# Two scales for the first range of w1, loaded and used half by half, in a two-phase MLP on one Trainium2 core

## The chip, the cores and the metric

The kernel runs on one core of a Trainium2 chip. The metric is the device time of one execution in microseconds (us). The kernel before the change took 1545.94, 1545.28 and 1545.81 us in three runs; the median is 1545.81.

## What is computed

Three float32 arrays go in: x (8 x 1024 x 1024, so 8192 rows of 1024), w1 (1024 x 4096) and w2 (4096 x 1024).

```python
h = x @ w1
h = 0.5 * h * (1 + np.tanh(np.sqrt(2 / np.pi) * (h + 0.044715 * h ** 3)))
return (h @ w2).astype(np.float32)
```

## The kernel before

**Engines.** TensorE (PE) does the matmuls, each with a 128x128 tile of weights. VectorE (DVE), ScalarE (ACT) and GpSimd (POOL) do everything between them, and SyncE (SP) issues most DMAs. Every engine works through its own instructions in the order in which the program gives them; the kernel uses a manual schedule, so this order is the order of the calls in the code. `V`, `S` and `G` are DVE, ACT and POOL, and `cast(eng, out, in, scale)` (L168-174) is a multiplication by a scale on one of the three.

**Data.** The 8192 rows are 64 chunks c of 128 rows, taken as 32 pairs k (chunks 2k and 2k+1). A chunk of x is loaded (`load_x`, L180), looked at by ACT for the sum of its absolute values in each row (`look_x`), given a scale `xm` and its inverse `xi` per row (`scale_x`), cast to f16 with it (`cast_x`, tile `x16`), and turned into `xT`. For the first twelve chunks TensorE does the turn (`turn_x_pe`, L204-218: eight matmuls into PSUM and a copy out by ACT or DVE); for the others a DMA does.

The columns of w1 are cut into four ranges r. A range has 512 columns in the left half of w1 (column block 0, in the code s=0) and 512 in the right half (block 1, s=1). It comes as eight tiles n of 128x2x512 float32: n0 to n3 hold block 0 (as B11 and B21), n4 to n7 block 1 (B12 and B22). Every tile is looked at (`look_w1`, L266), the maximum over the eight is taken per partition and written into a 128x128 tile `spread` (`widest_w1`), and a matmul called `rows` turns that, so that a reduction gives the maximum over all partitions (`all_partitions`, L154-160). From this come one scale `w1m`, its inverse `w1i` and `w1j` for the whole range (`scale_w1`, L278-282). Then `cast_w1` (L284-288) casts the eight tiles to f16 with `w1i`, and `sum_w1` (L290) forms the sums T1 to T4 of the four blocks B11, B21, B12, B22.

**First phase: gelu(x @ w1).** There are 128 units, one for each pair and range. The order (L576-578) takes the first six pairs (`FIRST`) through range 0, then through ranges 1, 2 and 3; then come 22 middle pairs, each with all four ranges, and the last four pairs range by range. Units 0 to 6 (pairs 0 to 5 with range 0, and pair 0 with range 1) are `Plain` (L426-443): four quarters of one half (128 rows) and one column block each, eight matmuls of 512 columns to a quarter. I call these quarters p0 to p27. The other units are `Quad1` (L445-503, called by `unit`, L694-732): seven products of four matmuls by Strassen's scheme, which need the sums of w1 above and four sums of the pair's `xT` (`sum_x`, L220-234, tile `xs`). In a unit, ACT and DVE copy and add PSUM banks into tiles `e`, ACT applies the gelu with a per-row factor `us`, POOL multiplies by a per-row factor `rs` and casts to f16 (tile `g`, L172), and SP stores `g` to DRAM (`gd`) some calls later (`held`, `let_go`). The two factors are products of the x scale and the scale of the range (`factors`, `factors_of_pair`).

**Second phase: g @ w2.** `second(n)` (L557-571) does the next n of 26 products per pair (eight matmuls of 256 columns each). Their left operands are tiles `gT`, loaded from `gd` by transposing DMAs (`load_g`), and sums `gs` of them on DVE (`sum_g`, L517). After a product ACT or DVE takes the PSUM bank into the output tile, once or twice (`take`, L522-544). The right operands are sums of w2 that the first phase computed, stored in DRAM and fetched again. w2's scale allows for the scales of the ranges of w1 (`widest_w2`, `scale_w2`), and `cast_w2` uses the entry of `w2s` of the range in question.

**Where the phases meet.** A `Quad1` unit finishes its last products in the next two calls of `unit`. In the calls for units 128 and 129 there is no new unit; there `extra(0)` stands in the place of product m1 and `extra(1)` in that of m5, and they call `second` for three and two products (L786) and for three and three (L787).

**Order of the other work.** All else (loads, looks, casts, sums) is put by hand into slots: `plan(u, slot, f)` has `f` called in unit u's slot 0 to 6, and `early(p, f)` (L594) plans for slot p % 4 of unit p // 4, that is, after quarter p. `background` calls what was planned. Each instruction then stands in its engine's queue behind all that was called before it.

**Start.** L740-773 loads x0, x1, the eight tiles of range 0 and x2 to x7 on SP's queue in that order; looks at, casts and turns x0 and x1; gives TensorE 30 warm-up matmuls of 256 columns (`warm_up`, L376, `WARM`), whose results nobody uses; looks at the eight tiles, runs `rows` and the scale, gives 16 more warm-ups, casts the eight tiles (six on DVE, two on ACT) and x2 and x3 on DVE; and then runs the seven plain units, with pair 0's quarters in the order of the column blocks and the other pairs' in that of the halves.

**Tiles.** `wpool` has 28 buffers of 4 KB per partition shared by raw and cast w1, early x and w2's products; `k2` has eleven for `e`, `x16`, `junk`, `g2` and `gs`; PSUM has three banks of each of `pa` and `pc` and two of `pb`, which the turns and `rows` use too.

Of the kernel before, what the change touches and what calls it, by code (L numbers as in the profile page):

```python
# [78 lines left out]
def kernel(  # L79
# [24 lines left out]
    WARM = 30  # L104
# [21 lines left out]
    w1a = small.tile([P, NR], F32, name="w1a")  # L126
    w1m = small.tile([P, NR], F32, name="w1m")
    w1i = small.tile([P, NR], F32, name="w1i")
    w1j = small.tile([P, NR], F32, name="w1j")
# [5 lines left out]
    w2s = small.tile([P, NR], F32, name="w2s")  # L135
    us = small.tile([P, NP, 2, NR], F32, name="us")
    rs = small.tile([P, NP, 2, NR], F32, name="rs")

    ones = small.tile([P, P], F32, name="ones")
# [11 lines left out]
    def spread_out(src):  # L151
        V.tensor_scalar(out=spread, in0=ones, scalar1=src, scalar2=None, op0=ALU.mult)
# [34 lines left out]
    def scale_x(c):  # L187
        V.tensor_scalar(
            out=xm[:, c:c + 1], in0=xl[:, c:c + 1], scalar1=2.0 ** -13, scalar2=TINY,
            op0=ALU.mult, op1=ALU.max,  # L190
        )
        V.reciprocal(xi[:, c:c + 1], xm[:, c:c + 1])
# [43 lines left out]
    def times(o, a, s):  # L236
        V.tensor_scalar(out=o, in0=a, scalar1=s, scalar2=None, op0=ALU.mult)
# [7 lines left out]

    def factors_of_pair(k):
        for h in range(2):
            times(us[:, k, h, :], w1m, xm[:, 2 * k + h:2 * k + h + 1])
            times(rs[:, k, h, :], w1j, xi[:, 2 * k + h:2 * k + h + 1])
# [24 lines left out]
    def widest_w1(r):  # L274
        V.tensor_reduce(out=w1a[:, r:r + 1], in_=w1c[:, r, :], op=ALU.max, axis=AX.X)
        spread_out(w1a[:, r:r + 1])

    def scale_w1(r):  # L278
        all_partitions(w1m[:, r:r + 1])
        V.tensor_scalar_max(w1m[:, r:r + 1], w1m[:, r:r + 1], TINY)  # L280
        V.reciprocal(w1i[:, r:r + 1], w1m[:, r:r + 1])
        V.tensor_scalar_mul(w1j[:, r:r + 1], w1i[:, r:r + 1], 1.0 / SPAN)

    def cast_w1(r, n, eng):  # L284
# [3 lines left out]
        cast(eng, w1set[r, b][:, 2 * half:2 * half + 2], wraw.pop((r, n)), w1i[:, r:r + 1])  # L288
# [23 lines left out]
    def widest_w2():  # L312
        V.tensor_reduce(out=w2m, in_=w2c, op=ALU.max, axis=AX.X)
        V.tensor_tensor(out=w2m, in0=w2m, in1=w1m, op=ALU.mult)
# [72 lines left out]
    class Out1:  # L387


        def begin(self, k, r):  # L390
            self.k, self.r = k, r
            self.u = [us[:, k, h, r:r + 1] for h in range(2)]
            self.v = [rs[:, k, h, r:r + 1] for h in range(2)]
# [6 lines left out]
        def gelu_pair(self, half, s, src):  # L400
            e = self.e()
            S.activation(out=e, in_=src, func=ACT.Gelu_apprx_tanh, scale=self.u[half])
# [3 lines left out]
            cast(G, g[:, s], e, self.v[half])  # L406
# [19 lines left out]
    class Plain(Out1):  # L426
# [4 lines left out]
        def run(self, banks, step):  # L431
            t = xT[self.k]
            for i, (half, s) in enumerate(((0, 0), (0, 1), (1, 0), (1, 1)) if self.k else ((0, 0), (1, 0), (0, 1), (1, 1))):
                ps = bank(banks[i])
                bs = (B12, B22) if s else (B11, B21)
                for j, b in enumerate(bs):
                    product(
                        ps, lambda n: t[:, half, j * HK + n, :],
                        [w1set[self.r, b][:, n, :] for n in range(HK)], j == 0,
                    )  # L440
                self.gelu_pair(half, s, ps)
                step(i)
                let_go(len(held) - 1 if len(held) > 1 and i % 2 else 0)
# [153 lines left out]
    for k in range(1, FIRST):  # L597
        for h in range(2):
            c = 2 * k + h
            if k > 1:  # L600
# [4 lines left out]
                if h:  # L605
                    early(p, factors, k, k + 1, 0)
# [87 lines left out]
    def unit(u, extra):  # L694
# [35 lines left out]
        if p1:  # L730
            p1.m4()
# [90 lines left out]
```

## Time and profile before

| | |
|---|---|
| three runs | 1545.94, 1545.28, 1545.81 us |
| the profiled execution | 1545.54 us |
| its span (first to last instruction) | 1543.8 us |
| PE busy | 1521.1 us (99% of the span), 10415 matmuls |
| PE weight loads | 1015.8 us (66%) |
| DVE busy | 1171.7 us (76%) |
| ACT busy | 731.5 us (47%) |
| POOL busy | 461.9 us (30%) |
| HBM | 97.0 MB read, 114.3 MB written, 137 GB/s over the span |

In the profile's rows a group reads: time or count, engine, line of the kernel, operation, tile written <- tiles read, partitions x elements and type, count. In brackets stands how long the engine had been idle just before and what ended that wait. Times are us from the start of the span unless they are durations. Matmul instructions that overlap with the next are counted once in busy time, so I judge TensorE by the distance from one start to the next. "Granted clock" 1.00 is TensorE's full speed as the records show it.

### The profile page before, as it was taken

How to read it: one execution, taken by the hardware profiler on the slowest of the kernel's cores; microseconds unless marked ns; L12 is line 12 of the kernel's file. 1: busy time of each engine (PE TensorE's matmuls, PEld its weight loads, DVE VectorE, ACT ScalarE, POOL GpSimd, SP SyncE). 2: the span in 40 equal slices, each digit the busy share in tenths (PEclk: the TensorE clock that was granted, in tenths of full speed). 3: DMA queues.
4: the chain of work that ended last, by engine and by line, in shares of the span. 5: the costliest groups of instructions: out<-in, count | busy, mean ns of one | idle time of the engine just before them, and what ended most of it. 6: DMA issues, size and time to landing. Idle time of an engine off the chain costs nothing.

```text
span 1543.8 us, 28585 instructions
## 1 busy us (share of the span) xinstructions
PE 1521.1 (99%) x10415; PEld 1015.8 (66%) x10415; DVE 1171.7 (76%) x2384; ACT 731.5 (47%) x1295; POOL 461.9 (30%) x568
## 2 busy tenths in 40 slices
PE   6999999999999999999999999999999999999999
PEld 4444444444444444444448888888888888888888
DVE  6787677777767776665238888888888888888886
ACT  6678777777777777797662111111111111111111
POOL 2767554466656665554442000000000000000000
PEclk9999999999999999999999999999999999999999
DMA  8654899878788887883799577668767766866872
GB/s 325 228 172 148 244 290 306 235 237 237 232 245 250 248 259 215 249 217 104 219 261 238 131 128 163 126 133 155 140 135 137 153 129 129 159 137 124 156 141 79
DMA packets 459804, 293.91 MB, mean 190 GB/s; under 512 B 333840, under 2 KB 427024, under 8 KB 459664
## 3 DMA queue, kind: packets, MB, share of 16 engines
q1 hardware_dynamic: 456208, 279.52, 71.4%
q0 software_dynamic: 3456, 12.58, 2.5%
q8 instruction: 81, 1.33, 0.4%
q14 instruction: 59, 0.48, 0.1%
HBM read 96.99 MB, written 114.29 MB: 137 GB/s over the span
## 4 chain that ended last, share of the span: by engine, by line
PE 94%; DMA 2%; DVE 2%; ACT 1%; issue 1%; POOL 0%; SPq 0%; ACTq 0%; POOLq 0%; DVEq 0%
PE pa L367 50%; PE pc L367 30%; PE pb L367 14%; DMA gd<-g 1%; DMA wn<-in_w_dram 1%; DVE e L163 0%; ACT w L170 0%; DVE w L166 0%; DMA xn<-in_x_dram 0%; DVE w1c L147 0%; POOL g L172 0%; DVE xs L166 0%; ACT e L414 0%; POOL wn L261 0%; PE turned L211 0%
## 5 line engine op out<-in xcount | busy, mean ns | idle before, releaser
L172 POOL TENSOR_SCALAR g<-e,rs 128x512 f16<-128x512 f32 x512 | 411.1, 814 | 355.6 <-ACT e L414 278.9
L367 PEld LDWEIGHTS <-gs 128*128 128x128 f16 x4608 | 450.7, 98 | 55.1 <-DVE gs L166 2.1
L367 PEld LDWEIGHTS <-xs 128*128 128x128 f16 x1936 | 189.3, 98 | 232.1 <-issue 2.8
L163 DVE TENSOR_TENSOR e<-pc,e 128x512 f32<-128x512 f32 x242 | 161.5, 686 | 213.4 <-ACT e L482 212.1
L367 PEld LDWEIGHTS <-xT 128*128 128x128 f16 x1676 | 163.5, 98 | 197.1 <-ACT xT L216 1.6
L367 PE MATMUL pa<-w,gs 128*128 128x256 f16 x2304 | 288.3, 273 | 1.1 <-DVE gs L166 1.1
L367 PE MATMUL pa<-w,xT 128*128 128x512 f16 x1080 | 255.7, 379 | 1.9 <-ACT xT L216 1.1
L414 ACT ACTIVATE e<-e,us 128x512 f32<-128x512 f32 x363 | 249.1, 719 | 7.7 <-DVE e L163 7.6
L367 PE MATMUL pa<-w,xs 128*128 128x512 f16 x968 | 248.4, 379 | 3.0 <-DVE xs L166 1.7
L367 PE MATMUL pc<-w,xs 128*128 128x512 f16 x968 | 248.4, 379 | 0.2 <-DVE e L163 0.2
L367 PEld LDWEIGHTS <-gT 128*128 128x128 f16 x2048 | 200.4, 98 | 23.2
L536 ACT ACTIVATE o<-pa,vo 128x256 f32<-128x256 f32 x96 | 45.2, 471 | 335.7 <-PE pa L367 333.2
L367 PE MATMUL pc<-w,gs 128*128 128x256 f16 x1536 | 194.0, 273 | 0.0
L367 PE MATMUL pa<-w,gT 128*128 128x256 f16 x1024 | 132.7, 273 | 0.0
L367 PE MATMUL pb<-w,xT 128*128 128x512 f16 x484 | 124.2, 379 | 0.0
L532 DVE SCALAR_TENSOR_TENSOR o<-pc,vo,o 128x256 f32<-128x256 f32 x160 | 77.1, 482 | 57.9 <-PE pc L367 57.9
L473 ACT COPY e<-pa 128x512 f32<-128x512 f32 x121 | 70.9, 586 | 89.8 <-PE pa L367 86.5
L166 DVE TENSOR_TENSOR gs<-gT,gs 128x1024 f16<-128x1024 f16 x160 | 109.4, 684 | 0.8 <-POOL g L172 0.5
L532 DVE SCALAR_TENSOR_TENSOR o<-pa,vo,o 128x256 f32<-128x256 f32 x192 | 92.1, 480 | 20.0 <-PE pa L367 19.7
L367 PE MATMUL pb<-w,gs 128*128 128x256 f16 x768 | 99.5, 273 | 0.4 <-DMA gd<-g 0.4
L367 PE MATMUL pc<-w,gT 128*128 128x256 f16 x768 | 99.5, 273 | 0.0
L463 ACT COPY e<-pa 128x512 f32<-128x512 f32 x121 | 69.9, 578 | 50.1 <-PE pa L367 50.1
(87 smaller groups left out, 1369.0 us busy)
## 6 DMA issues: line engine op xcount, KB each, us to landing
gd<-g SPq DMA_DIRECT2D x484, 128.0 KB, 2.9
wn<-in_w_dram SPq DMA_DIRECT2D x72, 512.0 KB, 5.5
xn<-in_x_dram SPq DMA_DIRECT2D x64, 512.0 KB, 5.3
out_dram<-o SPq DMA_DIRECT2D x62, 512.0 KB, 3.5
w<-wd SPq DMA_DIRECT2D x25, 512.0 KB, 6.2
wn<-in_w_dram POOLq DMA_DIRECT2D x24, 512.0 KB, 5.5
wd<-wt SPq DMA_DIRECT2D x24, 512.0 KB, 4.5
gd<-g SPq DMA_DIRECT2D x14, 256.0 KB, 4.7
```

What stands on the lines that cost most here:

```text
L163: V.tensor_tensor(out=o, in0=a, in1=b, op=ALU.add)
L166: V.tensor_tensor(out=o, in0=a, in1=b, op=ALU.subtract)
L172: G.tensor_scalar(out=o, in0=i, scalar1=s, scalar2=1.0, op0=ALU.mult, op1=ALU.mult)
L367: nc.tensor.matmul(bank, lhsT=left(i), rhs=right[i], start=start and i == 0, stop=i == n - 1, skip_group_check=True,)
L414: S.activation(out=e, in_=src, func=ACT.Gelu_apprx_tanh, scale=self.u[half])
L463: S.copy(self.e11, self.pa)
L473: S.copy(self.e12, self.pa)
L532: V.scalar_tensor_tensor(out=o, in0=ps, scalar=v, in1=o, op0=ALU.mult, op1=ALU.add)
L536: S.activation(out=o, in_=ps, func=ACT.Copy, scale=v)
```

## The change

- **Two scales.** Range 0 of w1 gets a scale for each column block. The arrays of w1's scales have two more columns (`NR` and `NR + 1`) for them; range 0's first six pairs use factors `up` and, for block 1, `rt` beside `rs`.
- **Start.** x0 and w1's n0 to n3 are loaded first, then x1 to x3, n4 to n7, x4 to x7. Only x0 is turned before the warm-ups, which are 26 and 12 instead of 30 and 16. Block 0 is scaled and cast alone (n0 and n2 on DVE, n1 and n3 on POOL), and quarters p0 to p3 take pairs 0 and 1 with block 0, p4 to p7 the same with block 1; the quarters after them run half by half, pair by pair. A function `between(p)`, called after the first four matmuls of a quarter, turns x1 and x2, looks at n4 to n7 (two on ACT), and in p3 runs the second `rows`, scale and casts (n4 and n6 on DVE, n5 and n7 on POOL). x3 is cast on POOL. The looks, scales and casts of pair 2's x are planned one quarter later; those of pairs 3 to 5 stay.
- **One scale afterwards.** `join_w1` (after quarter 10) takes the larger of the two scales as that of the range and its ratio to each block's. `even_w1` multiplies the cast blocks by that ratio in place, eight casts of 128x1024 f16 on POOL in units 17 to 20, slots 2 and 5; `sum_w1` of range 0 comes one unit later. The middle and last pairs' `factors_of_pair` get a fifth operation for `rt`, since block 1's `w1j` for that range is its own column, and `cast_w2` picks the column of the block.
- **The tile `ones` is gone:** `spread` is made from `identity` (times 0, plus the maximum).
- **Pair 0's x sums** move from unit 11, slots 2 to 5, to units 8 and 9, slots 0 and 1.
- **The meeting.** In units 128 and 129 three products of the second phase follow the slot of g11 and `let_go`, and three follow m4; before, they stood at the places of m1 and m5, three and two or three and three.

The diff, without the resized tiles and with small changes (functions that only take a count or an engine more, or another column) cut:

```diff
@@ -101,7 +102,7 @@
     LAST = 4
-    WARM = 30
+    WARM = 26
@@ -149,7 +152,9 @@
     def spread_out(src):
-        V.tensor_scalar(out=spread, in0=ones, scalar1=src, scalar2=None, op0=ALU.mult)
+        V.tensor_scalar(
+            out=spread, in0=identity, scalar1=0.0, scalar2=src, op0=ALU.mult, op1=ALU.add
+        )
@@ -243,10 +251,17 @@
 
+    def factors_of_block(k, block, eng):
+        c, b = slice(2 * k, 2 * k + 2), slice(NR + block, NR + block + 1)
+        times(up[:, block, c], xm[:, c], w1m[:, b], eng)
+        times(rt[:, c] if block else rs[:, k, :, 0], xi[:, c], w1j[:, b], eng)
...
-            times(us[:, k, h, :], w1m, xm[:, 2 * k + h:2 * k + h + 1])
-            times(rs[:, k, h, :], w1j, xi[:, 2 * k + h:2 * k + h + 1])
+            times(us[:, k, h, :], w1m[:, :NR], xm[:, 2 * k + h:2 * k + h + 1])
+            times(rs[:, k, h, :], w1j[:, :NR], xi[:, 2 * k + h:2 * k + h + 1])
+        times(rt[:, 2 * k:2 * k + 2], xi[:, 2 * k:2 * k + 2], w1j[:, NR + 1:NR + 2])
@@ -271,21 +286,40 @@
 
-    def widest_w1(r):
-        V.tensor_reduce(out=w1a[:, r:r + 1], in_=w1c[:, r, :], op=ALU.max, axis=AX.X)
-        spread_out(w1a[:, r:r + 1])
-    def scale_w1(r):
-        all_partitions(w1m[:, r:r + 1])
-        V.tensor_scalar_max(w1m[:, r:r + 1], w1m[:, r:r + 1], TINY)
-        V.reciprocal(w1i[:, r:r + 1], w1m[:, r:r + 1])
-        V.tensor_scalar_mul(w1j[:, r:r + 1], w1i[:, r:r + 1], 1.0 / SPAN)
+    def widest_w1(r, block=None):
+        c, src = (r, w1c[:, r, :]) if block is None else (NR + block, w1c[:, r, 4 * block:4 * block + 4])
+        V.tensor_reduce(out=w1a[:, c:c + 1], in_=src, op=ALU.max, axis=AX.X)
+        spread_out(w1a[:, c:c + 1])
+    def scale_w1(c):
+        c = slice(c, c + 1)
+        all_partitions(w1m[:, c])
+        V.tensor_scalar_max(w1m[:, c], w1m[:, c], TINY)
+        inverse_w1(c)
+    def inverse_w1(c):
+        V.reciprocal(w1i[:, c], w1m[:, c])
+        V.tensor_scalar_mul(w1j[:, c], w1i[:, c], 1.0 / SPAN)
+    def join_w1():
+        V.tensor_tensor(out=w1m[:, :1], in0=w1m[:, NR:NR + 1], in1=w1m[:, NR + 1:], op=ALU.max)
+        V.reciprocal(w1i[:, :1], w1m[:, :1])
+        times(ratio, w1m[:, NR:], w1i[:, :1])
+        V.tensor_copy(out=w1j[:, :1], in_=w1j[:, NR:NR + 1])
+    def even_w1(b, half):
+        t = w1set[0, b][:, 2 * half:2 * half + 2]
+        block = b in (B12, B22)
+        cast(G, t, t, ratio[:, block:block + 1])
...
-        cast(eng, w1set[r, b][:, 2 * half:2 * half + 2], wraw.pop((r, n)), w1i[:, r:r + 1])
+        c = r or NR + n // 4
+        cast(eng, w1set[r, b][:, 2 * half:2 * half + 2], wraw.pop((r, n)), w1i[:, c:c + 1])
@@ -389,8 +423,13 @@
             self.k, self.r = k, r
-            self.u = [us[:, k, h, r:r + 1] for h in range(2)]
-            self.v = [rs[:, k, h, r:r + 1] for h in range(2)]
+            c = lambda h: slice(2 * k + h, 2 * k + h + 1)
+            self.u = [[us[:, k, h, r:r + 1]] * 2 for h in range(2)]
+            self.v = [[rs[:, k, h, r:r + 1]] * 2 for h in range(2)]
+            if not r:
+                self.v = [[self.v[h][0], rt[:, c(h)]] for h in range(2)]
+            if not r and k < FIRST:
+                self.u = [[up[:, s, c(h)] for s in range(2)] for h in range(2)]
@@ -399,11 +438,11 @@
             e = self.e()
-            S.activation(out=e, in_=src, func=ACT.Gelu_apprx_tanh, scale=self.u[half])
+            S.activation(out=e, in_=src, func=ACT.Gelu_apprx_tanh, scale=self.u[half][s])
...
-            cast(G, g[:, s], e, self.v[half])
+            cast(G, g[:, s], e, self.v[half][s])
@@ -411,9 +450,9 @@
         def gelu(self, half, s, e, src):
-            S.activation(out=e, in_=src, func=ACT.Gelu_apprx_tanh, scale=self.u[half])
+            S.activation(out=e, in_=src, func=ACT.Gelu_apprx_tanh, scale=self.u[half][s])
             g = k1.tile([P, N], F16, name="g", tag="k1")
-            cast(G, g, e, self.v[half])
+            cast(G, g, e, self.v[half][s])
@@ -428,19 +467,17 @@
 
-        def run(self, banks, step):
+        def quarter(self, half, s, which, between):
             t = xT[self.k]
-            for i, (half, s) in enumerate(((0, 0), (0, 1), (1, 0), (1, 1)) if self.k else ((0, 0), (1, 0), (0, 1), (1, 1))):
-                ps = bank(banks[i])
-                bs = (B12, B22) if s else (B11, B21)
-                for j, b in enumerate(bs):
-                    product(
-                        ps, lambda n: t[:, half, j * HK + n, :],
-                        [w1set[self.r, b][:, n, :] for n in range(HK)], j == 0,
-                    )
-                self.gelu_pair(half, s, ps)
-                step(i)
-                let_go(len(held) - 1 if len(held) > 1 and i % 2 else 0)
+            ps = bank(which)
+            for j, b in enumerate((B12, B22) if s else (B11, B21)):
+                product(
+                    ps, lambda n: t[:, half, j * HK + n, :],
+                    [w1set[self.r, b][:, n, :] for n in range(HK)], j == 0,
+                )
+                if not j:
+                    between()
+            self.gelu_pair(half, s, ps)
@@ -594,25 +631,28 @@
 
-    for k in range(1, FIRST):
+    early(1, turn_x_pe, 3, S)
+    for k in range(2, FIRST):
...
-            if k > 1:
-                p = (3, 7, 11, 14)[k - 2] + h
-                early(p - 1, look_x, c)
-                early(p, scale_x, c)
-                early(p, cast_x, c, V)
-                if h:
-                    early(p, factors, k, k + 1, 0)
+            p = (4, 7, 11, 14)[k - 2] + h
+            early(p - 1, look_x, c)
+            early(p, scale_x, c)
+            early(p, cast_x, c, V)
+            if h:
+                early(p, factors_of_block, k, 0, V)
+                early(p, factors_of_block, k, 1, G)
...
-            early(4 * k - 2 + 2 * h, turn_x_pe, c, V if h or k == 1 else S)
+            early(4 * k - 2 + 2 * h, turn_x_pe, c, V if h else S)
...
+            elif k:
+                plan(FIRST + k - 1, 2 + i, sum_x, k, (i,))
             else:
-                plan(FIRST + (k - 1) % FIRST, 2 + i, sum_x, k, (i,))
+                plan(FIRST + 2 + i // 2, i % 2, sum_x, k, (i,))
@@ -643,8 +683,12 @@
             plan(u + 5 + i // 2, (4, 6, 1, 3)[i], sum_w1, r, t)
+    early(10, join_w1)
+    for i, b in enumerate((B12, B11, B22, B21)):
+        for half in range(2):
+            plan(3 * FIRST - 1 + i, (2, 5)[half], even_w1, b, half)
     for i, t in enumerate((T1, T3, T2, T4)):
-        plan(3 * FIRST + i, 5, sum_w1, 0, t)
+        plan(3 * FIRST + 1 + i, 5, sum_w1, 0, t)
@@ -697,8 +741,6 @@
             q.m1()
-        else:
-            extra(0)
@@ -707,6 +749,8 @@
         let_go(len(held) - 2 if len(held) > 2 else 0)
+        if u >= NQ:
+            extra()
@@ -724,11 +768,11 @@
             q.m5()
-        else:
-            extra(1)
...
+        if u >= NQ:
+            extra()
@@ -737,45 +781,69 @@
     ):
-        for c in range(2):
-            load_x(c, wpool, "w")
-        for n in range(8):
+        load_x(0, wpool, "w")
+        for n in range(4):
             load_w1(0, n)
-        V.memset(ones, 1.0)
...
-        for c in range(2, 8):
+        for c in range(1, 4):
             load_x(c, wpool, "w")
-        for c in range(2):
+        for n in range(4, 8):
+            load_w1(0, n)
+        for c in range(4, 8):
+            load_x(c, wpool, "w")
+        look_x(0)
+        scale_x(0)
+        cast_x(0, S)
+        t = x16[0]
+        turn_x_pe(0, S)
+        warm_up(t, WARM)
+        for n in range(4):
+            look_w1(0, n)
+        widest_w1(0, 0)
+        for c in range(1, 4):
             look_x(c)
-            if c:
-                for n in range(3):
-                    look_w1(0, n)
-            scale_x(c)
-            cast_x(c, S)
-            t = x16[c]
-            turn_x_pe(c, S)
-        warm_up(t, WARM)
-        for n in range(3, 8):
-            look_w1(0, n)
-        widest_w1(0)
-        scale_w1(0)
-        warm_up(t, 16)
-        for n in (0, 1, 2, 3, 4, 5):
-            cast_w1(0, n, S if n in (2, 3) else V)
-        factors(0, 1, 0)
-        for c in (2, 3):
-            look_x(c)
-        for c in (2, 3):
-            cast_w1(0, c + 4, V)
-            scale_x(c)
-            cast_x(c, V)
-        factors(1, 2, 0)
-        for u in range(FIRST + 1):
-            Plain(*order[u]).run(
-                ("pa", "pc", "pa", "pc"),
-                lambda i: [background(u, j) for j in ((i,) if i < 3 else (3, 4, 5, 6))],
-            )
+        scale_w1(NR)
+        warm_up(t, 12)
+        cast_w1(0, 0, V)
+        cast_w1(0, 1, G)
+        scale_x(1)
+        cast_x(1, V)
+        cast_w1(0, 3, G)
+        cast_w1(0, 2, V)
+        factors_of_block(0, 0, G)
+        plain = {(k, 0): Plain(k, 0) for k in range(FIRST)}
+        plain[0, 1] = Plain(0, 1)
+        quarters = [(k, 0, half, s) for s in range(2) for k in range(2) for half in range(2)]
+        quarters += [(k, 0, half, s) for k in range(2, FIRST) for half in range(2) for s in range(2)]
+        quarters += [(0, 1, half, s) for half in range(2) for s in range(2)]
+        def between(p):
+            if p == 0:
+                turn_x_pe(1, V)
+                look_w1(0, 4, S)
+                scale_x(2, 2)
+                cast_x(2, V)
+                cast_x(3, G)
+                factors_of_block(1, 0, G)
+            elif p == 1:
+                turn_x_pe(2, V)
+                look_w1(0, 5, S)
+                look_w1(0, 6)
+                look_w1(0, 7)
+                widest_w1(0, 1)
+            elif p == 3:
+                scale_w1(NR + 1)
+                for n in (4, 5, 6, 7):
+                    cast_w1(0, n, G if n % 2 else V)
+                for k in range(2):
+                    factors_of_block(k, 1, V)
+        for p, (k, r, half, s) in enumerate(quarters):
+            plain[k, r].quarter(half, s, ("pa", "pc")[p % 2], lambda: between(p))
+            for j in (p % 4,) if p % 4 < 3 else (3, 4, 5, 6):
+                background(p // 4, j)
+            let_go(len(held) - 1 if len(held) > 1 and p % 2 else 0)
@@ -783,8 +851,8 @@
         V.tensor_scalar(out=vn, in0=vo, scalar1=-1.0, scalar2=None, op0=ALU.mult)
-        unit(NQ, lambda i: second(3 - i))
-        unit(NQ + 1, lambda i: second(3))
+        for u in range(NQ, NQ + 2):
+            unit(u, lambda: second(3))
```

More of the change, by code (lines that the diff above doesn't have):

```diff
@@ L125 @@
     w1c = small.tile([P, NR, 8], F32, name="w1c")
[L126 to L129, printed above, removed]
+    w1a = small.tile([P, NR + 2], F32, name="w1a")
+    w1m = small.tile([P, NR + 2], F32, name="w1m")
+    w1i = small.tile([P, NR + 2], F32, name="w1i")
+    w1j = small.tile([P, NR + 2], F32, name="w1j")
     w2c = small.tile([P, NR, 2 * JR], F32, name="w2c")
@@ L134 @@
     w2i = small.tile([P, 1], F32, name="w2i")
-    w2s = small.tile([P, NR], F32, name="w2s")
+    w2s = small.tile([P, NR + 2], F32, name="w2s")
     us = small.tile([P, NP, 2, NR], F32, name="us")
     rs = small.tile([P, NP, 2, NR], F32, name="rs")
-    ones = small.tile([P, P], F32, name="ones")
+    rt = small.tile([P, T // P], F32, name="rt")
+    up = small.tile([P, 2, 2 * FIRST], F32, name="up")
+    ratio = small.tile([P, 2], F32, name="ratio")
     spread = small.tile([P, P], F32, name="spread")
@@ L185, in look_x, with scale_x @@
         S.activation(out=junk, in_=xraw[c], func=ACT.Abs, accum_out=xl[:, c:c + 1])
-    def scale_x(c):
+    def scale_x(c, n=1):
         V.tensor_scalar(
-            out=xm[:, c:c + 1], in0=xl[:, c:c + 1], scalar1=2.0 ** -13, scalar2=TINY,
+            out=xm[:, c:c + n], in0=xl[:, c:c + n], scalar1=2.0 ** -13, scalar2=TINY,
             op0=ALU.mult, op1=ALU.max,
         )
-        V.reciprocal(xi[:, c:c + 1], xm[:, c:c + 1])
+        V.reciprocal(xi[:, c:c + n], xm[:, c:c + n])
     def cast_x(c, eng):
@@ L234, in sum_x, with times @@
                 sub(s[:, 0], a12, s[:, 2])
-    def times(o, a, s):
-        V.tensor_scalar(out=o, in0=a, scalar1=s, scalar2=None, op0=ALU.mult)
+    def times(o, a, s, eng=V):
+        if eng is G:
+            G.tensor_scalar(out=o, in0=a, scalar1=s, scalar2=1.0, op0=ALU.mult, op1=ALU.mult)
+        else:
+            V.tensor_scalar(out=o, in0=a, scalar1=s, scalar2=None, op0=ALU.mult)
     def factors(k0, k1, r):
@@ L313, in widest_w2 @@
         V.tensor_reduce(out=w2m, in_=w2c, op=ALU.max, axis=AX.X)
-        V.tensor_tensor(out=w2m, in0=w2m, in1=w1m, op=ALU.mult)
+        V.tensor_tensor(out=w2m, in0=w2m, in1=w1m[:, :NR], op=ALU.mult)
         V.tensor_reduce(out=w2a, in_=w2m, op=ALU.max, axis=AX.X)
@@ L334, in cast_w2 @@
             w2u[c, j // 2] = k4.tile([P, 2, 4, Q], F16, name="wu", tag="k4")
-        r = (8 * j + c) % IK // JR
+        r = (8 * j + c) % IK // JR or NR + j // 2
         o = w2u[c, j // 2][:, j % 2].rearrange("p n q -> p (n q)")
```

## The prediction

> **What bounds the kernel now.** I read the busy time by stretch first. The columns are stretch, length, then busy time and instructions of TensorE, its weight loads, VectorE (DVE), ScalarE (ACT) and GpSimd (POOL), then granted clock, DMA share, GB/s.
>
> ```profile
> 0.00:20.44 20.44, 8.11 (x63) 6.61 (x64) 12.51 (x22) 8.67 (x10) 0.70 (x6) 1.00 0.93 350
> 20.44:118.00 97.56, 93.53 (x491) 44.34 (x489) 76.47 (x136) 72.08 (x117) 65.71 (x77) 1.00 0.64 217
> 118.00:806.00 688.00, 687.64 (x3188) 311.82 (x3186) 462.78 (x1040) 527.71 (x905) 385.36 (x476) 1.00 0.78 232
> 806.00:820.00 14.00, 11.75 (x86) 8.05 (x84) 10.99 (x20) 6.41 (x13) 8.81 (x8) 1.00 1.05 277
> 820.00:1543.80 723.80, 720.12 (x6595) 645.01 (x6592) 608.95 (x1170) 116.67 (x253) 1.36 (x2) 1.00 0.71 141
> ```
>
> TensorE sets the time; its products number the same after the change. What can be won is its idle time: 20.44 us before the first product, 97.56 - 93.53 = 4.03 up to 118, 14.00 - 11.75 = 2.25 at the meeting of the phases. The middle has 0.36. Next, the timeline of the start:
>
> ```profile
> 4.30 1.06 ACT L185 ACTIVATE junk<-xn 128x1024 bf16<-128x1024 f32 x1 [2.28 <-DMA xn<-in_x_dram]
> ...
> 13.42 4.33 PE L379 MATMUL pb<-x 128*128 128x256 f16 x30
> ...
> 18.53 0.30 PE L157 MATMUL rows<-identity,spread 128*128 128x128 f32 x1 [0.77 <-DVE spread L152]
> ...
> 20.44 2.12 PE L367 MATMUL pa<-w,xT 128*128 128x512 f16 x8
> ...
> 30.20 1.89 PE L367 MATMUL pc<-w,xT 128*128 128x512 f16 x8
> ```
>
> x0 has landed at 4.30. `rows` turns the per-partition maxima; the scale of w1 and every cast hang on it. At 30.20 quarter p5 starts, with p0 to p4 and the turns of x0 to x3 done; the changed kernel has the same behind it at its p5, so I compare p5's starts. Then TensorE's waits between 50 and 118, and at the meeting:
>
> ```profile
> 52.70 1.90 PE L367 MATMUL pa<-w,xT 128*128 128x512 f16 x8 [1.11 <-ACT xT L216]
> ...
> 108.34 1.04 PE L367 MATMUL pa<-w,xs 128*128 128x512 f16 x4 [1.72 <-DVE xs L166]
> ...
> 113.03 1.02 PE L367 MATMUL pc<-w,xs 128*128 128x512 f16 x4 [0.20 <-DVE e L163]
> ```
>
> ```profile
> 808.01 1.04 PE L367 MATMUL pc<-w,gs 128*128 128x256 f16 x8
> 809.48 1.05 PE L367 MATMUL pb<-w,gs 128*128 128x256 f16 x8 [0.43 <-DMA gd<-g]
> ...
> 812.96 1.04 PE L367 MATMUL pc<-w,gT 128*128 128x256 f16 x8
> 814.68 1.02 PE L367 MATMUL pa<-w,xT 128*128 128x512 f16 x4 [0.69 <-ACT e L482]
> 815.54 1.04 PE L367 MATMUL pa<-w,gs 128*128 128x256 f16 x8
> 817.71 1.05 PE L367 MATMUL pa<-w,gs 128*128 128x256 f16 x8 [1.12 <-DVE gs L166]
> ```
>
> Eight 256-wide matmuls take 0.87 us start to start, four 512-wide ones 0.86. So the meeting loses 0.60 + 0.85 + 1.30 = 2.75 us. Last, casts on two engines at once:
>
> ```profile
> 60.15 1.41 DVE L174 TENSOR_SCALAR w<-wn,w1i 128x1024 f16<-128x1024 f32 x2
> 60.30 2.40 POOL L172 TENSOR_SCALAR g<-e,rs 128x512 f16<-128x512 f32 x2
> ```
>
> Two such POOL operations need 1.36 us alone (at 123.39); here 2.40, for they stood until DVE's two casts had ended at 61.56. **DVE and POOL casts don't overlap.** The changed start puts half of its w1 casts on POOL.
>
> **The start, step by step.** (1) Loads. The chain of waits has x1 landing at 5.57 and the eighth w1 load at 5.59 + 11.03 = 16.62: 1.38 us each. With x0 first and four w1 loads behind it, the fourth lands at 4.28 + 4 x 1.38 = 9.8. From the last landing to `rows` it took 18.53 - 16.62 = 1.91 (reduce, maximum, spread), so `rows` could run at 11.7. (2) `rows` now stands behind 26 warm-ups, which start after x0's turn, at 7.9, instead of after x1's at 13.42. In the profile they went 213 ns start to start up to 15.2, 2.65 us after the turn of x1 began at 12.59, and 109 ns from then on. All 26 at 109 end at 10.7, in time; all at 213 at 13.4, 1.7 late. I take `rows` at R = 12.4, near the middle, since one rise of the clock is all that is shown. (3) `rows` to the inverse scale took 1.01 (18.53 to 19.54). Then p0 needs w1 casts n0 and n2 and x1's cast on DVE (0.67 apart in the row of four at 19.64) and n1 and n3 on POOL (1.11, at 62.69): one after another 4.2; then 0.1 and up to 0.86 of matmuls. p0 ends at R + 1.05 + 4.2 + 0.96 = R + 6.2. (4) From there ACT loads its table (1.28, at 23.86), makes e (0.6), looks at w5 (1.15), makes e (0.6) and copies x3's turn (1.0): p3 starts 4.7 later, 0.3 after TensorE could. Half of p3 (0.86), the second `rows` and inverse (1.0), four casts in turn (2 x 0.67 + 2 x 1.11 = 3.55), 0.55 to p4's end: 10.7 in all. **p5 starts at R + 16.9 = 29.3, 0.9 sooner than 30.20.** Ends: R from 11.7 to 13.4, and 0.7 later where POOL casts x3 before DVE casts x2: 28.6 to 31.0. Were casts to overlap, p0 would end at R + 3.9 and the second four take 2.2: p5 at 25.0 to 26.7. I keep -5.2 to +0.8 as bounds and take -0.9, by the row at 60.15. The loads aren't the bound after w3: w7 lands near 19, its look ends near 22, and p3 asks for it near 24.
>
> The clock's row shows 2.65 us from first work to full speed. [...]
>
> **Other edits.** Pair 0's x sums leave unit 11 for units 8 and 9. There DVE stood idle 0.38 and 1.50 us before its adds at 81.72 and 87.01, which holds four sums of 0.33. In unit 11 they were what TensorE waited for at 108.34; by start to start that wait and those at 113.03 and 114.87 are 1.88 + 0.36 + 0.12. Next due is w1's T2 of range 2, ready at 105.81, asked for at 106.46. **-2.1** (0 to -2.4: DVE's 3.28 us stall at 99.66 behind POOL's run stays). One `rows` more, 0.1; the spread in unit 8 ended 0.23 before `rows` and gets one sum more ahead of it, 0.1.
>
> The meeting: T3's product of unit 127 goes ahead of the three first of phase two, so the one that waited at 809.48 stands 0.86 later: 0.60 gone. ACT copies e22 before it takes products, so T4 no longer waits: 0.85 gone. But the next sums on DVE reuse buffers that POOL frees; its fourth g of that run ended at 812.53, so the fourth product, due at 812.3, may wait up to 1.0, and the seventh stands behind four DVE operations (0.6 each), 0.9 to 1.0. Of 2.75, 0.9 to 2.0 stay: **-1.2** (-1.8 to -0.7).
>
> Eight casts on POOL even out the blocks in units 17 to 20, 1.11 to 2.2 each by POOL's rows. POOL is idle 3.3 of 6.04 us in a unit from 150 on, but backed up from 136 to 147. DVE, in order, stands behind POOL there; the adds free PSUM. **+0.3** (0 to 9.4, below). A tiny factor more for 26 pairs is 0.23 us each on DVE, which idles a third of that stage; if that cover went, 6 us of DVE, not TensorE. Three tiny POOL factors sit under quarters of 1.73. The wait at 52.70 is a store's landing (41.49 to 48.32) and keeps its distance to TensorE: 0 (+-0.7). Two loads of x go sooner, into a queue that was idle at 26 to 28.
>
> Sum: -0.9 - 2.1 - 1.2 + 0.2 + 0.3 = -3.7. The profiled execution took 1545.54, span 1543.8 and 1.74 around; the median of the runs shown is 0.27 above it. Forecast 1545.81 - 3.7 = **1542.1**.
>
> **Rivals.** (a) *Casts overlap at the start.* For it: the row at 60.15 is of other sizes, and small steps lie between. p5 at 25.8 instead of 29.3: 1538.6. (b) *Another wait replaces the one at 108.34,* since POOL's back-to-back run from 98.48 to 104.5 stays and holds DVE; or `rows` comes at 13.4 and the start gives nothing. Either takes 1 to 2.1 back: 1544.0. (c) *Slower: POOL starves DVE.* In units 17 to 20 the new casts make POOL run back to back again. The one such run in the profile (98.48 to 104.5) cost 2.4 us of TensorE; four units of it cost 9.4: 1542.1 - 0.3 + 9.4 = 1551.2. It decides once the backlog outlasts a unit, so that e tiles aren't free for ACT's copies; two such units already spoil the gain. Against it: at 136 to 147 POOL was full without a wait on TensorE.
>
> **How the numbers follow.** A difference under 0.2% (3.1 us) can't be told from none. Forecast 60% (1540.5 to 1544.0; 46 of it below 1542.7, 14 within 0.2%); (a) 14%, faster; (b) 18%, within; (c) 8%, slower. Faster 0.60, same 0.32, slower 0.08. The range runs from (a) with 0.4 to spare, 1538.2, to 1545.8, past (b) with the bounds of the start; (c) and part of the tails are left out.
>
> **What would show it.** Right: the first `rows` at 12 to 13, POOL's first w1 casts well over 1.11 us or DVE's over 0.75, p5 near 29.3; no wait of TensorE for x sums near 107; one or two waits on DVE sums of 0.5 to 1 us near 811 to 817. Wrong: p5 before 27 or after 31; DVE operations of 2 us and more with TensorE waits between 133 and 158; a new wait of over 2 us anywhere before 118.

## The result

The changed kernel takes 1543.16 us (median of 22 runs, 1541.29 to 1544.39), the one before 1545.44 (22 runs beside them, 1544.57 to 1546.38). The ratio is 0.9985, with a 95% interval of 0.9979 to 0.9992: 2.3 us, or 0.15%, faster. The forecast was 3.7 us. The interval leaves out 1, so this difference under 0.2% could be told from none. The range of its first case, 1540.5 to 1544.0, holds the time, but what it held likeliest, faster by over 0.2%, did not come; the gain lies within 0.2%, where rival (b) stood.

The profiled execution took 1542.97 us with a span of 1541.1. Its busy time by stretch, in the columns shown for the kernel before, the first stretch again up to the first product:

```profile
0.00:14.20 14.20, 6.57 (x47) 5.19 (x48) 7.30 (x15) 6.89 (x9) 1.50 (x7) 1.00 0.88 327
14.20:118.00 103.80, 96.84 (x506) 45.50 (x506) 85.50 (x148) 74.17 (x120) 80.06 (x97) 1.00 0.68 231
118.00:806.00 688.00, 687.63 (x3188) 311.81 (x3186) 470.62 (x1066) 528.34 (x905) 395.82 (x481) 1.00 0.79 233
806.00:820.00 14.00, 12.80 (x104) 10.00 (x103) 11.95 (x23) 6.62 (x13) 10.10 (x9) 1.00 0.99 256
820.00:1541.10 721.10, 717.32 (x6568) 642.22 (x6566) 606.11 (x1164) 115.54 (x251) 0.69 (x1) 1.00 0.71 140
```

The first product starts 6.24 us sooner, but the stretch up to 118 now has 6.96 us without TensorE (4.03 before). The middle is as full as it was, 0.37 idle, though POOL does 10.5 us more in it. At the meeting 1.20 are idle where 2.25 were, and the last stretch has 3.78 (3.68). Next, the timeline of the start:

```profile
12.28 0.30 PE L162 MATMUL rows<-identity,spread 128*128 128x128 f32 x1
...
13.40 3.18 POOL L177 TENSOR_SCALAR w<-wn,w1i 128x1024 f16<-128x1024 f32 x2 [12.08 <-DVE w1i L302]
13.40 0.74 DVE L179 TENSOR_SCALAR w<-wn,w1i 128x1024 f16<-128x1024 f32 x1
...
15.52 1.60 DVE L179 TENSOR_SCALAR w<-wn,w1i 128x1024 f16<-128x1024 f32 x1
...
17.18 1.02 PE L401 MATMUL pa<-w,xT 128*128 128x512 f16 x4 [0.90 <-DVE w L179]
...
28.46 1.89 PE L401 MATMUL pc<-w,xT 128*128 128x512 f16 x8
```

`rows` runs at 12.28, two POOL casts take 3.18 (2.22 alone), DVE's second 1.60 (0.67 alone), and p5 starts at 28.46, 1.74 sooner than before. Then TensorE's waits in the rest of the execution:

```profile
51.85 1.90 PE L401 MATMUL pa<-w,xT 128*128 128x512 f16 x8 [2.00 <-ACT xT L221]
...
107.07 1.02 PE L401 MATMUL pa<-w,xs 128*128 128x512 f16 x4 [1.02 <-ACT e L500]
...
814.57 1.03 PE L401 MATMUL pa<-w,gs 128*128 128x256 f16 x8 [1.20 <-ACT o L573]
...
831.54 1.05 PE L401 MATMUL pa<-w,gT 128*128 128x256 f16 x8 [0.22 <-DMA w<-wd]
832.81 1.05 PE L401 MATMUL pc<-w,gs 128*128 128x256 f16 x8 [0.23 <-DMA w<-wd]
```

By start to start these are 2.16 (1.28 before), 1.18 (2.35 in three waits), 1.36 (2.74 in three), 0.39 and 0.39 (new). The wait near 51 grew, the one near 107 has another releaser, ACT's copy instead of the x sums, and the last two are for products of w2 fetched from DRAM. The wait near 51 isn't the same in every execution: the five profiles whose program doesn't differ from the changed kernel's up to there have 1.58 to 2.16, 1.89 on average, the three with the old start 1.07 to 1.28. What holds ACT ahead of the first two waits, in ACT's timeline:

```profile
47.56 0.69 ACT L441 ACTIVATE e<-pc,up 128x512 f32<-128x512 f32 x1 [1.71 <-DMA gd<-g]
...
105.82 0.72 ACT L453 ACTIVATE e<-e,us 128x512 f32<-128x512 f32 x1 [1.01 <-DVE e L168]
106.45 0.57 ACT L500 COPY e<-pa 128x512 f32<-128x512 f32 x1
```

The first waits 1.71 us for a store of g to land, since its tile e takes that store's buffer. The second waits for DVE's add, and the copy that TensorE needs stands behind it. DVE and POOL at the same place:

```profile
100.40 3.05 DVE L171 TENSOR_TENSOR w<-w 128x2048 f16<-128x2048 f16 x1 [0.93 <-POOL w L177]
103.38 0.68 DVE L168 TENSOR_TENSOR e<-pc,e 128x512 f32<-128x512 f32 x1
103.98 1.21 DVE L171 TENSOR_TENSOR w<-w 128x2048 f16<-128x2048 f16 x1
105.11 0.68 DVE L168 TENSOR_TENSOR e<-pc,e 128x512 f32<-128x512 f32 x1
```

```profile
97.92 2.45 POOL L177 TENSOR_SCALAR w<-wn,w1i 128x1024 f16<-128x1024 f32 x1
100.36 3.65 POOL L177 TENSOR_SCALAR g<-e,rs 128x512 f16<-128x512 f32 x4
```

```profile
102.36 1.65 POOL L177 TENSOR_SCALAR g<-e,rs 128x512 f16<-128x512 f32 x1
```

A sum that takes DVE 1.21 at 103.98 takes 3.05 at 100.40, beside POOL's four casts, after 0.93 of waiting for POOL's cast of w1 n6. The last line is the fourth of these casts alone: it took 1.65, the three ahead of it 0.68 to 0.69 each, as they do alone. So the sum stood until the third had ended, and then the fourth stood until the sum had.

### The profile page after: what moved, and what is told of

The parts are those of the page before. It is cut to its first block, busy times and chain, and to the rows that moved or that the text cites. A ratio compares the mean times of both kernels' runs of the same rounds, so it can differ in the third digit from the quotient of the medians.

```text
span 1541.1 us, 28626 instructions
## 1 busy us (share of the span) xinstructions
PE 1521.2 (99%) x10408; PEld 1014.7 (66%) x10408; DVE 1181.5 (77%) x2413; ACT 731.6 (47%) x1296; POOL 488.2 (32%) x593
## 5 line engine op out<-in xcount | busy, mean ns | idle before, releaser
L177 POOL TENSOR_SCALAR g<-e,rs 128x512 f16<-128x512 f32 x448 | 366.1, 827 | 279.6 <-ACT e L453 240.2
```

What stands on the lines that cost most here:

```text
L177: G.tensor_scalar(out=o, in0=i, scalar1=s, scalar2=1.0, op0=ALU.mult, op1=ALU.mult)
```

## The experiments

All profiles in one table. A wait is what a distance from start to start exceeds the usual one (216 ns for 512 columns, 109 for 256, 56 for 128), counted from 60 ns; columns 4 to 8 are sums of them in us between the times named. The last matmul is that of the profiled execution; times are medians, with the number of runs, and the ratio is to the kernel before on the same chip.

| kernel | `rows` | p5 | 45-56 | 100-116 | 145-200 | 800-820 | 820-850 | last matmul | time (runs) | ratio, 95% |
|---|---|---|---|---|---|---|---|---|---|---|
| before | 18.53 | 30.20 | 1.28 | 2.35 | 0 | 2.74 | 0 | 1539.84 | 1545.44 (22) | 1 |
| changed | 12.28 | 28.46 | 2.16 | 1.18 | 0 | 1.36 | 0.78 | 1537.49 | 1543.16 (22) | 0.9985 (0.9979-0.9992) |
| start alone | 12.73 | 28.89 | 2.06 | 2.32 | 0 | 2.59 | 0 | 1539.50 | 1544.66 (10) | 0.9990 (0.9981-0.9999) |
| sums alone | 19.03 | 30.67 | 1.07 | 1.18 | 0 | 2.99 | 0 | 1539.42 | 1544.59 (10) | 0.9991 (0.9982-1.0000) |
| meeting alone | 19.08 | 30.72 | 1.23 | 2.31 | 0 | 1.49 | 0.67 | 1539.71 | 1545.12 (10) | 0.9993 (0.9983-1.0003) |
| casts on DVE | 12.62 | 28.76 | 1.20 | 1.23 | 0 | 1.31 | 0 | 1537.02 | 1542.46 (1) | |
| later loads | 11.70 | 27.86 | 0.72 | 1.18 | 0 | 2.81 | 0 | 1536.64 | 1542.14 (7) | 0.9974 (0.9962-0.9987) |
| n6 on DVE | 13.12 | 29.27 | 1.73 | 0 | 0 | 1.59 | 0 | 1536.35 | 1541.80 (1) | |
| evening twice | 11.90 | 28.04 | 1.94 | 1.23 | 3.89 | 1.92 | 0.22 | 1541.68 | 1547.16 (1) | |
| three edits | 11.94 | 28.09 | 0.59 | 0 | 0 | 2.69 | 4.26 | 1539.27 | 1541.55 (8) | 0.9971 (0.9961-0.9981) |
| four edits | 12.96 | 29.10 | 0.74 | 0 | 0 | 2.69 | 1.19 | 1537.40 | 1541.38 (12) | 0.9972 (0.9964-0.9981) |
| fetches ahead | 12.87 | 29.01 | 1.58 | 1.23 | 0 | 2.56 | 0 | 1538.42 | 1544.14 (1) | |

A single time says little here: the changed kernel's runs alone lie 3.1 us apart. The waits carry the verdicts.

**Start alone.** The changed kernel with the two other parts undone:

```diff
-            elif k:
-                plan(FIRST + k - 1, 2 + i, sum_x, k, (i,))
             else:
-                plan(FIRST + 2 + i // 2, i % 2, sum_x, k, (i,))
+                plan(FIRST + (k - 1) % FIRST, 2 + i, sum_x, k, (i,))
```

and `extra(0)`, `extra(1)` at the places of m1 and m5 as before.

> The changed kernel with pair 0's x sums and the meeting's order as before: the start, the two scales and the evening casts stay. Theory (the parts add up in TensorE's waits): p5 starts at 28.5 as in the changed kernel, the wait near 51.8 is 2.2 us (1.3 before), so of the 1.74 us won at the start 0.85 stay; the second `rows` and the new spread cost 0.27; the waits for x sums near 107 are 1.9 + 0.4 + 0.1 and those at the meeting 2.7 in all, as before. The last product comes 0.6 us sooner than before, the time is about 1544.8. Rival (the parts interact: an earlier start only shifts DVE and POOL against each other): the waits near 107 differ from before by over 0.5 us, and the time is 1543.2 or 1545.4.

**Sums alone.** The kernel before with the last lines of that diff the other way round.

> The kernel before with nothing but pair 0's x sums moved from unit 11 to units 8 and 9. Theory (POOL's back-to-back run holds DVE, and DVE's late add holds ACT's copies): the waits at 113 and 114.9 are gone, and at 107.9 stays a wait of 1.2 us, now for ACT's copy out of PSUM instead of for the x sums; 1.2 us won, about 1544.3. Rival (the wait of 1.18 us that the changed kernel has there comes from its other start or from the join of the scales): no wait over 0.3 us there, 2.1 to 2.4 won, about 1543.2.

**Meeting alone.** The kernel before with `extra()` after the slot of g11 and after m4, three products each.

> The kernel before with nothing but the new order at the meeting. Theory (the order itself makes the new waits): of 2.74 us one wait of 1.4 stays, near 817, and two waits of 0.4 for fetched products of w2 appear near 834 and 835, since these fetches stand on SP's queue behind four transposing loads and TensorE comes to them sooner: 0.6 us won, about 1544.8. Rival (the two waits come from all that was won earlier in the program, not from the meeting): no wait between 825 and 840, 1.4 won, about 1544.0.

The theory held in all three: 2.06 near 52 and 2.32 near 107 with the start alone; 1.18 near 108 with the sums alone, again after a DVE sum of 3.05; a wait of 1.38 near 817 and a new one of 0.67 at 835 with the meeting alone (one fetch instead of two). The start alone had `rows` 0.45 us later than the changed kernel's profile, and its last matmul is 0.34 ahead of before instead of 0.6. The two others have the old start, and yet `rows` 0.50 and 0.55 later than the profile before. So I compare from p5 to the last matmul: against 1509.64 before, the start alone takes 0.97 more, the sums alone 0.89 less, the meeting alone 0.65 less, 0.57 less in all; the changed kernel takes 0.61 less. In TensorE's waits the parts add up. The times can't tell: the three ratios add up to 0.26%, the changed kernel has 0.15%, and each interval is about 0.1% either way.

**Casts on DVE.** The changed kernel with

```diff
-        cast_w1(0, 1, G)
+        cast_w1(0, 1, V)
...
-        cast_w1(0, 3, G)
+        cast_w1(0, 3, V)
...
-                    cast_w1(0, n, G if n % 2 else V)
+                    cast_w1(0, n, V)
```

> The changed kernel with the four casts of range 0 that it gives POOL at the start on DVE. Theory (casts on DVE and POOL don't overlap, so that only the sum of their times counts): before p0's second half five DVE casts of 0.67 and the scale of x1 take 3.7 us from the inverse scale, as the mixed row does (13.40 to 17.12), so p0 ends as it does now; the second four take 2.7 instead of 3.2, and p5 starts at 28.0 (28.46 now). Rival (they overlap in part, so that one engine alone takes longer): p0's second half starts 0.6 us or more later than 17.18, p5 after 28.7.

Its timeline, DVE doing all eight (x1's cast stands between the first two rows):

```profile
13.72 1.41 DVE L179 TENSOR_SCALAR w<-wn,w1i 128x1024 f16<-128x1024 f32 x2
...
16.09 1.42 DVE L179 TENSOR_SCALAR w<-wn,w1i 128x1024 f16<-128x1024 f32 x2
...
25.19 3.09 DVE L179 TENSOR_SCALAR w<-wn,w1i 128x1024 f16<-128x1024 f32 x4
```

From `rows` to p5 it takes 16.14 us here and 16.14 with the four edits, where DVE casts too; 16.14 to 16.18 in the seven profiles where POOL shares the casts. So one engine or two make no difference of 0.05 us. The expected 28.0 was wrong: `rows` came 0.34 later, and the second four casts took 3.09 instead of 2.7, since a cast of g on POOL, 1.62 long there, stood beside the fourth. By its letter p5 at 28.76 is past the rival's 28.7, but from `rows` on nothing is later. The wait near 51, 1.20, is shorter than in the runs with POOL's casts; why wasn't followed up. That the two engines work in turn is seen in the changed kernel's rows of the first casts, each alone (DVE's two are shown above):

```profile
13.40 1.65 POOL L177 TENSOR_SCALAR w<-wn,w1i 128x1024 f16<-128x1024 f32 x1 [12.08 <-DVE w1i L302]
14.44 1.16 DVE L179 TENSOR_SCALAR x<-xn,xi 128x1024 f16<-128x1024 f32 x1
15.03 1.54 POOL L177 TENSOR_SCALAR w<-wn,w1i 128x1024 f16<-128x1024 f32 x1
```

The casts end at 14.14 (DVE), 15.05 (POOL), 15.60 (DVE), 16.58 (POOL) and 17.12 (DVE). In this exchange POOL's add 0.9 to 1.0 each and DVE's about 0.55, less than the 1.11 and 0.67 of casts that stand alone.

**Later loads.** The changed kernel with

```diff
-        early((3, 4, 6, 7, 8, 9, 10, 11)[n], load_w1, 1, n)
+        early((3, 4, 6, 7, 8, 10, 11, 12)[n], load_w1, 1, n)
```

> The changed kernel with w1's tiles n5, n6 and n7 of range 1 loaded one quarter later each (after quarters 10, 11 and 12 instead of 9, 10 and 11). Theory (the store of g that holds ACT at 45.8 to 47.5 is late because it stands behind a w1 load issued at 40.42, 0.09 us ahead of it): the store lands before 46, ACT doesn't wait for it, and of the wait of 2.16 us near 51.8 at most 0.5 is left, what ACT's own looks and copies make: 1.7 us sooner from there to the end, about 1541.4. Rival 1 (ACT's looks and copies are what holds TensorE there): 1.5 us or more stay. Rival 2 (the later loads hold up range 1's scale or casts): a new wait of over 1 us between 53 and 76.

ACT's row there is

```profile
45.42 0.69 ACT L441 ACTIVATE e<-pc,up 128x512 f32<-128x512 f32 x1 [0.18 <-PE pc L401]
```

The wait near 50 fell from 2.16 to 0.63, with 0.08 more at 53.7; ACT's gelu waits 0.18 for TensorE, not for a store. The store was issued at 39.91 and landed at 45.33, 5.4 us later; in the changed kernel it was issued at 40.51 and landed at 47.47, 7.0 later. In the nine profiles where the load goes ahead this store took 6.1 to 7.0, in the three with the later loads 4.1 to 5.7. No new wait stands between 54 and 74. So the store was late because of the load ahead of it, though POOL issues the loads and SP the stores. But the last matmul came only 0.85 sooner, though `rows` too was 0.58 sooner. The waits from 800 to 850 are 0.67 more than in the changed kernel, and four small ones after 870 that it hasn't, of 0.09 to 0.12, add up to 0.45. The first new one stands at 806.84, and these lines of TensorE, POOL and DVE show where it comes from:

```profile
806.84 1.05 PE L401 MATMUL pb<-w,gs 128*128 128x256 f16 x8 [0.72 <-DVE gs L171]
```

```profile
805.36 6.36 POOL L177 TENSOR_SCALAR g<-e,rs 128x512 f16<-128x512 f32 x6 [4.27 <-DMA gd<-g]
```

```profile
806.09 0.69 DVE L171 TENSOR_TENSOR gs<-gs,gT 128x1024 f16<-128x1024 f16 x1 [1.89 <-POOL g L177]
```

POOL waits for stores that land at 805.21 and 805.54, DVE's sum for a buffer from POOL, TensorE for the sum: 0.88 from start to start. In the changed kernel these stores landed at 805.74 and 806.07, when TensorE was 2.0 us later, and it didn't wait.

**n6 on DVE.** The changed kernel with

```diff
-            plan(v, 3 + n % 4 * (n < 6), cast_w1, r, n, S if n % 2 else G)
+            plan(v, 3 + n % 4 * (n < 6), cast_w1, r, n, S if n % 2 else V if (r, n) == (2, 6) else G)
```

> The changed kernel with one cast of w1 (range 2, tile n6, in unit 10) on DVE instead of POOL; POOL's cast of it stood at 97.92 and took 2.45 us, and DVE's sum of w1 waited for it until 100.40 and then took 3.05. Theory (POOL's back-to-back run holds DVE): DVE casts it in 0.7 to 1.2, its next sum doesn't wait, the adds that free PSUM come 2 us sooner, and the wait of TensorE near 107 falls from 1.18 to 0.3 or less. Rival (DVE has too much to do in units 10 and 11, whoever runs beside it): with 0.7 to 1.2 more on DVE the wait near 107 stays at 1.2 or grows to 2.

```profile
97.11 0.90 DVE L179 TENSOR_SCALAR w<-wn,w1i 128x1024 f16<-128x1024 f32 x1
...
100.23 1.21 DVE L171 TENSOR_TENSOR w<-w 128x2048 f16<-128x2048 f16 x1
101.37 0.68 DVE L168 TENSOR_TENSOR e<-pc,e 128x512 f32<-128x512 f32 x1
```

```profile
98.29 6.03 POOL L177 TENSOR_SCALAR g<-e,rs 128x512 f16<-128x512 f32 x4
```

The wait near 107 is gone altogether, with more work on DVE. The sum takes 1.21 and the add that frees PSUM starts 2.0 sooner. The price falls on POOL: its four casts of g now take 6.03 instead of 3.65, and no wait of TensorE follows from it. Whether it was POOL's cast ahead of the sum or the four behind it that mattered most isn't told apart; one edit changed both.

**Evening twice.** The changed kernel with `for _ in range(2):` around the cast of `even_w1`.

> The changed kernel with each of the eight evening casts done twice (the block with the smaller scale is multiplied by its ratio twice, so that the later pairs' part of range 0 is off by that ratio). POOL then has 4 x 1.12 + 4 x 0.68 = 7.2 us of work in units of 6.04, on top of the run from 133 to 142. Theory (a backlog of POOL costs TensorE only once it outlasts the e tiles; the casts that are there stay under that point): about 9 us more of backlog by 162, which is past it: waits of TensorE of 3 to 9 us in all between 145 and 175. Rival (the tiles hide even that): no wait over 0.5 us there, the time as the changed kernel's.

TensorE's timeline there:

```profile
162.06 1.02 PE L402 MATMUL pa<-w,xs 128*128 128x512 f16 x4 [0.37 <-ACT e L501]
171.11 1.89 PE L402 MATMUL pa<-w,xT 128*128 128x512 f16 x8 [0.87 <-ACT e L520]
174.75 1.02 PE L402 MATMUL pa<-w,xs 128*128 128x512 f16 x4 [1.75 <-ACT e L511]
```

3.89 us of waits between 162 and 178, all for ACT's copies, and ACT's longest wait there is one of 2.6 us for POOL's g. With one set of casts POOL works without a pause from 133 to 167 and costs TensorE nothing; with two it does, from 162 on.

**Three and four edits.** Later loads, n6 on DVE, and two fetches of w2's products ahead of the four transposing loads; the fourth edit is that of the casts on DVE.

```diff
-        plan(at[last[0]] + (r + 1) * LAST + (r < 3) + (n > 4), n, fetch_w2, node)
+        plan(at[last[0]] + (r + 1) * LAST + (r < 3) + (n > 4), n * (i not in (22, 23)), fetch_w2, node)
```

> The changed kernel with three edits at once: w1's n5 to n7 of range 1 loaded one quarter later, the cast of n6 of range 2 on DVE, and two of the four last fetches of w2's products put ahead of the four transposing loads on SP's queue. Theory (the waits add up, each with its own cause): near 51 at most 0.7 us of 2.16 left, near 107 none of 1.18, none for fetched products near 831: 3.4 us less than the changed kernel in TensorE's waits, of which up to 0.7 may come back in the wait for the first sums at the meeting (0.88 in the run with the later loads); 1539.7 to 1540.5. Rival (the meeting's DMA queues, full from 780 on, set the end: who comes sooner waits longer): all over 1 us of the gain is lost between 800 and 840, 1541.5 or more.

> The same three edits and the four casts of range 0 at the start on DVE instead of POOL. Theory (no overlap, so the start's sum is the same; POOL comes free sooner for the first g): p5 from the inverse scale within 0.2 us of the changed kernel's, the wait near 51 no longer than with the three edits; 1539.3 to 1540.5. Rival (as for the three edits): lost at the meeting, 1541.5 or more.

> The changed kernel with two of the four last fetches of w2's products planned in slot 0 of unit 128, ahead of the four transposing loads on SP's queue. Theory (the waits of 0.39 us each at 831.5 and 832.8 come from these fetches standing behind the transposing loads): both are gone, the rest of the meeting stays at 1.4: 0.8 us less than in the changed kernel's profile. Rival (DMA engines are full there, whatever the order): waits of 0.3 us or more stay between 825 and 840, for the fetches or for the loads now behind them.

Up to 130 both sets of edits did what was expected: 0.6 and 0.7 near 50, none near 107. Then the rival held in the profiles: 2.69 at the meeting, and 4.26 and 1.19 after it. The timelines of TensorE and DVE and two stretches of the three edits show the largest:

```profile
832.06 1.16 PE L401 MATMUL pa<-w,gT 128*128 128x256 f16 x8 [2.45 <-DVE o L569]
```

```profile
830.52 0.69 DVE L171 TENSOR_TENSOR gs<-gT,gs 128x1024 f16<-128x1024 f16 x1 [3.83 <-DMA gT<-gd]
```

```profile
826.00:832.00 6.00, 3.61 (x34) 3.09 (x32) 2.17 (x6) 0.00 (x0) 0.00 (x0) 1.00 1.06 275
832.80:836.20 3.40, 3.40 (x18) 2.36 (x17) 2.82 (x7) 0.00 (x0) 0.00 (x0) 0.50 0.30 119
```

DVE waits 3.83 for the last transposing load, TensorE 2.61 for DVE (start to start), and then the granted clock is 0.50 for 3.4 us, which costs 1.65 more. SP's queue tells why the load is late:

```profile
811.77 14.41 SPq L548 DMA_TRANSPOSE gT<-gd  x4
```

In the run with the later loads the four took 11.03 from 811.62. Where the two fetches stand ahead (three, four edits, fetches ahead) the last of them lands at 830.4, 828.7 and 830.6; without, at 827.2 and 825.7 (changed, later loads). From the first one's issue to the last one's landing that is 16.1 to 18.7 us with the fetches ahead, 13.6 and 14.1 without. With the four edits the wait of 1.19 at 832.65 isn't settled: a fetch that stands behind the transposing loads landed at 832.60, and a take of DVE's ended at 832.61. With the fetches ahead alone there is no wait near 831.5 and 832.8. But three runs that leave the fetches in their place (casts on DVE, later loads, n6 on DVE) have none there either, so it isn't shown that this edit removed them; and 1.12 of waiting stand at 809 in its profile. A gain of that edit isn't shown. The profiled execution of the three edits was the slowest of its eight (1544.70; the fastest took 1539.66), so its 4.26 is probably not the usual case. By the medians the three and four edits are the fastest, 1541.55 and 1541.38 (the theory had 1539.3 to 1540.5, the rival 1541.5 or more), next to 1542.14 with the later loads alone. All three are faster than the kernel before; than the changed one by 1.0 to 1.8 us in the medians and 0.11 to 0.14% in the ratios, with intervals that overlap. For the later loads and n6 on DVE together without the moved fetches, and for stores of g ahead of fetches at the meeting, there is no measured time, so what causes the loss at the meeting is argued from these profiles and stays open.

## Why the prediction was right and where it failed

- **The bound:** right. Outside the half-rate stretch of the three edits the products keep their spacing, and the gain is the change of TensorE's waits: 1.74 sooner at p5, then 7.59 us of waits after it instead of 8.15 (all of them, those near 77, 84, 94 and 132 too), makes 2.30 of the 2.35 us between the last matmuls. By the sum's own terms: -1.74 (start), +0.88 (the wait at 52.70), -1.17 (x sums), +0.27 (`rows` and spread), -0.60 (meeting), 0 (evening). That the start's surplus of 0.84 and the loss of 0.88 behind it cancel was not foreseen, and it is in part luck that the time lies in the range; the 1.4 us that are missing are those of the x sums and the meeting.
- **Start, steps 1 and 2** (`rows` at R = 12.4, between 11.7 and 13.4): right; 12.28 in this profile, 11.70 to 13.12 in nine with the new start, 12.46 on average. In eight of the nine `rows` follows the start of the last of the 26 warm-ups by 0.11 us, so warm-ups, not loads, set it there. The changed kernel's own profile is the ninth: its spread, behind the loads and looks, ended at 12.14 (11.43 to 11.71 in the others), after the warm-ups. The half rate (warm-ups 213 ns apart from start to start, 109 behind it) lasted until 2.75 to 5.5 us after the first matmul, a spread of 2.8 us over the nine profiles; what sets its length isn't shown. Fewer warm-ups were not tried.
- **Start, steps 3 and 4** (p5 at R + 16.9): the mechanism right, the size off. The casts run in turn, as the ends of the single casts show, and the run with all of them on DVE takes as long (16.14 us from `rows` to p5); rival (a), p5 at 25.0 to 26.7, is out. But in turn they cost less than the sum of their times alone: the first five took 3.7 instead of 4.2, DVE's small operations on x1's scale beside POOL's cast included, and the second four 3.18 instead of 3.55. So p0 ends at R + 5.8 instead of 6.2, and p5 starts at R + 16.15 on average. With R that is -1.74 instead of -0.9. The three profiles with the old start have p5 at 30.20 to 30.72, the nine with the new one at 27.86 to 29.27; the averages are 1.9 apart.
- **"The wait at 52.70 is a store's landing and keeps its distance to TensorE: 0 (+-0.7)":** failed. The store was issued 0.98 sooner, behind a w1 load 0.09 ahead of it, landed 0.85 sooner, and TensorE came 1.74 sooner: 0.88 of the start's gain were given back there. By the averages above it is 0.7. With the load put off, 0.7 are left of 2.16. The wait as it stands, 2.16, is past the 2 us that the prediction named as a sign of being wrong, though it is an old wait that grew and not a new one.
- **x sums, -2.1:** failed by half. That DVE stayed late behind POOL's run was seen, but what is "next due" was sought among w1's sums only, at 106.46. Due as well was the add ahead of ACT's gelu and copy. That is rival (b), by its own mechanism, and it left 1.18; moving one cast from POOL to DVE took all of it away (0 in the three profiles with that edit).
- **`rows` and spread, +0.2:** 0.27 in unit 8; it is there with the sums alone and not with the start alone, so it comes of the sums put ahead of the spread.
- **The meeting, -1.2:** -0.60 in this profile, 1.36 + 0.78 left of 2.74. The wait at 809.48 and that for T4 went, and the seventh product waits, but 1.36 instead of 0.9 to 1.0: DVE's sums ahead of it ended at 814.43, as thought of, and ACT's take of the bank at 814.52. The fetches behind four transposing loads weren't in the list. Over the six profiles with this order and the fetches in their place 1.3 to 2.8 are left, 2.0 on average; over the three with the old order 2.6 to 3.0 stand.
- **The evening casts, +0.3:** 0. POOL ran back to back from 133 to 167 as feared in rival (c), and TensorE didn't wait. Doubled casts cost 3.89, so the mechanism is real; where between one set and two it starts isn't shown.

## What to carry to other kernels

An operation that ends sooner is worth only what the next waits leave of it: here a store's landing took back half of the start's gain (0.88 of 1.74 us), and with the later loads, where the DMA share at the meeting is 1.03 (800 to 820), 0.7 of what was won near 50 was lost again there. With n6 on DVE nothing of what was won near 107 was. When a wait goes, list everything due in the next few microseconds on every engine in between (adds and copies that free buffers too), and not only the next operand. A second engine for casts won nothing here, where the two work in turn (16.14 to 16.18 us from `rows` to p5 with both, 16.14 with DVE alone); time the pair together first.

## What was not expected of the hardware

- After a pause of 2.61 us in TensorE (829.4 to 832.1 with the three edits) the granted clock fell to 0.50 at 832.8 and stayed there for 3.4 us; the pause of 2.16 at 51.85 in the changed kernel, and all shorter ones behind p5 in the twelve profiles, didn't do that (clock 1.00).
- The warm-up's length varied: the same matmuls ran at half rate (213 ns apart instead of 109) until 2.75 to 5.5 us after the first, so the start of one and the same program varied by 1.4 us (`rows` at 11.70 to 13.12).
- POOL was slowed by DVE too, not only DVE by POOL (a sum of 1.21 took 3.05 in the changed kernel): four casts of 0.68 took 3.65 beside that sum, and 6.03 beside a run of DVE sums with n6 on DVE.
